# First diff head projected ahead of the remaining differential values, rotary tables placed by transposes, in a two-layer decoder trunk

## The chip, the core and the metric

The kernel runs on one core of a Trainium2 chip. Its engines work side by side, each through its own instructions in order: TensorE (PE) multiplies matrices, VectorE (DVE), ScalarE (ACT) and GpSimd (POOL) do the rest, and SyncE (SP) issues nearly all DMA transfers; ACT can issue transfers too. An engine that waits for another holds up all that stands behind the waiting instruction. The metric is the device time of one execution in microseconds (us).

## The reference, cut to what matters

```
rotary_tables: ang = positions[..., None] * inv_freq          # 8 frequencies
               cos, sin = cos(ang), sin(ang)
partial_rotary(t): t1, t2, rest = t[..., :8], t[..., 8:16], t[..., 16:]
               concat([t1*cos - t2*sin, t2*cos + t1*sin, rest])
for l in range(2):
    h = rms_norm(x, attn_pre_g[l]);  proj = h @ w_in[l]
    qa, ka, va, qb, kb, vb, f_logit = split(proj)
    qa, ka = partial_rotary(qa), partial_rotary(ka)            # 4 diff heads, 2 maps of 64 each
    oa = rms_norm(diff_attention(qa, ka, va, lam), diff_sub_g[l]) * (1 - lam_init)
    ob = forgetting_attention(qb, kb, vb, cumsum(log_sigmoid(f_logit + bias)))   # 8 fox heads
    x = x + rms_norm(concat(oa, ob) @ w_out[l], attn_post_g[l])
    h = rms_norm(x, ffn_pre_g[l])
    x = x + rms_norm((silu(h @ w_gate[l]) * (h @ w_up[l])) @ w_down[l], ffn_post_g[l])
```

x is 512 tokens by 1024, a head has 64 dims, the feed-forward width is 2816; everything is float32.

## The kernel before

Each float32 factor is split into a rounded part `h` and a remainder `l`, and a product is three matmuls, h by h, h by l and l by h. The split costs a copy on ACT (`hi`) and a subtraction on DVE or POOL (`lo`). The normalised input stands transposed in `hT_h` and `hT_l`, in eight blocks `k` of 128 columns.

Layer 0 starts in `start()`. Four token tiles `t` of 128 rows are loaded (`xs`), squared and summed, scaled by POOL's `r_s` (`h_a`, L483), transposed on PE (`hp_a`, L209) in two halves `z` and split into `hT`. Beside that the weights of the differential values `va` come in four chunks `c` of two blocks (`w_load`), and PE computes `va` in 16 pieces (t, c) of six matmuls. `WARM` small matmuls on zeros stand ahead of and between the first pieces. The raw weights lie in the later `mixed_d` and in `raw_v`, the split ones in the places of the first queries and keys (`qs`, `ks` tiles) and of a weight chunk (`wh`, `wl`).

`tables()` makes the rotary tables `cosT` and `sinT`, one row for each of the 128 dims of a map pair: eight loads put the positions (L541), a chain of small DVE instructions on 128 x 32 elements brings the angles into range (L550 to L563), ACT takes the sines (L565, L566), and the result goes to DRAM (`tab_d`, L570) and back into the rows of the tables (L575). It also loads the mask (`con`), the triangle `tu` that becomes `upr`, and the lambda vectors `lv`.

Then come the heads. `tile_chunk` loads and splits the weights of one head's keys or queries (`wr_kd`, `wh_kd`, `wl_kd`; `q` for queries, `f` for a fox pair), projects them on PE (`pj_kd`, 24 matmuls), and for a diff head rotates them: DVE multiplies by `cosT` (t1, L728), shuffles (L732) and multiplies by `sinT` (t2, L735), POOL adds (L738); ACT and DVE or POOL split the sum into `qs` or `ks` (L697, L705, L706), and two transfers copy the key halves (L710). `diff_head` computes scores `sd` (two matmuls each), softmax on DVE, ACT and POOL, transposes `ptd`, and the product with the values `od`. `fox_head` does alike with a decay.

The order is not written by hand in this part. Every step is an `Op` with an engine, an assumed duration, a key and the buffers that it takes and gives; `Plan.run` picks for each engine the ready step with the lowest key, or else the one that can start first, and the instructions are emitted in that order. Projections have the key `FILLER` and so fill PE wherever no step of a head is ready. `va` pieces have the keys

```
done[t, c] = add("P", 1390, vas, hT[t, c // 2] + wl[c] + ([done[t, c - 1]] if c else []),
                 key=500 + VA_C * c + VA_T * t)
```

so that all of them run ahead of any projection. The transfers stand on SP's queue in a fixed order (`order="ld"`), and a transfer that takes over one of eight completion semaphores waits for the transfer that had it before.

Of the kernel before, what the change touches and what calls it, by code (L numbers as in the profile page):

```python
# [34 lines left out]
TB = S // 16  # L35
VA_C, VA_T = 4, 1
# [7 lines left out]
C_ID, C_M, C_F, NKEEP, C_U = 0, 128, 640, 641, 641  # L44
NCONST = 1153
# [113 lines left out]
def _constants():  # L159

    c = np.zeros((P, NCONST), np.float32)
    r = np.arange(P)
    c[:, C_ID:C_ID + P] = np.eye(P, dtype=np.float32)
    c[:, C_U:C_U + P] = (r[None, :] >= r[:, None]).astype(np.float32)
    c[:, C_U + P:C_U + S] = 1.0
    c[:, C_M + S - P:C_M + S] = np.where(r[None, :] > r[:, None], np.float32(-BIG), np.float32(0.0))
    expo = np.arange(0, ROT, 2, dtype=np.float32) / np.float32(ROT)
    inv_freq = (np.float32(1.0) / np.power(np.float32(500000.0), expo).astype(np.float32)).astype(np.float32)
    c[:, C_F] = inv_freq[r // 16]
    return c  # L170
# [3 lines left out]
def hymba_block(ctx, tc, x_d, pos_d, apre_d, win_d, fb_d, lq1_d, lk1_d, lq2_d, lk2_d, dsg_d, wout_d, apost_d,  # L174
# [64 lines left out]
    V.memset(sinT, 0.0)  # L239
    G.memset(cosT, 1.0)  # L240
# [102 lines left out]
    for l in range(DEPTH):  # L343
        win = win_d[l]
        with ExitStack() as actx:
# [12 lines left out]
            mixed_d = ap.tile([P, NDIFF, S], F32, name=f"mixd{l}", tag="v8", bufs=5)  # L358
            if l == 0:
                raw_v = ap.tile([P, NDIFF, S], F32, name=f"rawv{l}", tag="v8", bufs=5)  # L360
# [18 lines left out]
            vd, tab = [], []  # L379
# [12 lines left out]

            def start():

                plan.free.update(g=[], v8=[0.0], qs=[], ks=[])
# [9 lines left out]
                idd = dma(con[:, :P], con_d[:, :P], P)  # L405

                def w_load(c):
                    raw = (mixed_d, raw_v)[c // 2][:, 2 * (c % 2):2 * (c % 2) + 2]
                    if c == 0:
                        dst = q_tile("wva0h"), q_tile("wva0l")  # L410
                    elif c < 3:
                        w = k_tile(f"wva{c}")
                        dst = w[:, 0], w[:, 1]
                    else:
                        dst = [wpool.tile([P, WCH], F32R, name=f"{x}_va3", tag=x).rearrange("p (a b) -> p a b", a=2)
                               for x in ("wh", "wl")]
                    hi, lo = dst
                    d = dma(raw, win[2 * c * P:(2 * c + 2) * P, VA:VA + S].rearrange("(k p) n -> p k n", p=P), 2 * S)
                    ops = []
                    for k in range(2):  # L420
                        wva[2 * c + k] = hi[:, k], lo[:, k]
                        a = add("A", dA(S), lambda k=k: A.copy(hi[:, k], raw[:, k]), [d], key=-85 + c,
                                take=["w"] if c == 3 and k == 0 else [], order="hi w" if c == 3 and k == 0 else "")
# [13 lines left out]
                zeros = sinT.bitcast(mybir.dt.bfloat16)  # L437
# [16 lines left out]
                for t in range(NT):  # L454
# [24 lines left out]
                    for z in range(2):  # L479
# [20 lines left out]
                        p = add("P", 436, tr, [v, idd], key=key, take=["ts"[z]], give=["e"])  # L500
# [3 lines left out]
                for t in range(NT):  # L504
                    for c in range(4):
                        def vas(t=t, c=c):
                            if t == NT - 1:
# [4 lines left out]
                                         key=500 + VA_C * c + VA_T * t)  # L512
                    vd_split(t, [done[t, 3]])
                for c in range(4):
                    add("P", 0, lambda: None, [done[t, c] for t in range(NT)], key=-99,
                        give=(["qs", "qs"], ["ks"], ["ks"], ["w"])[c])
                add("P", 0, lambda: None, wl[2] + wl[3], key=-99, give=["v8"])
                add("P", 0, first_va.clear, [done[t, 0] for t in range(NT)], key=-99)
                return hT[NT - 1, 1]

            def tables(last):

# [3 lines left out]
                tab_d = dpool.tile([4, 8, S], F32, name="tab_d", tag="tabd")  # L526
# [4 lines left out]
                def get(dst, src, n, **kw):  # L531
                    return add("Q", max(400, 1.43 * n), lambda: nc.sync.dma_start(dst(), src), key=1, lat=2000,
                               order="ld" + "".join(f" {k}" for k in kw.get("take", ())), **kw)

                def positions():
                    w = rbuf("rd", F32, "rot")
                    x["p"] = w[:, :TB].bitcast(I32)
                    x["a"], x["n"] = w[:, TB:2 * TB], w[:, 2 * TB:3 * TB]
                    x["t"] = w[:, 4 * TB:8 * TB].rearrange("p (x j) -> p x j", x=4)
                    blocks = pos_d[0].rearrange("(b j) -> b j", j=TB)  # L540
                    return [lambda f=f: nc.sync.dma_start(x["p"][16 * f:16 * f + 16], blocks) for f in range(8)]  # L541

                def sums():
                    x["tu"] = rbuf("rc", F32, "tu")
                    return x["tu"]
# [4 lines left out]
                v = op("V", 100, lambda: V.tensor_copy(x["a"], x["p"]), [dp])  # L550
                v = op("V", 100, lambda: V.tensor_scalar_mul(x["a"], x["a"], con[:, C_F:C_F + 1]), [v, dc])
                for sc in (2.0 ** 22, 2.0 ** 11, 1.0):
                    v = op("V", 100, lambda sc=sc: V.tensor_scalar(
                        x["n"], x["a"], scalar1=1.0 / (2.0 * math.pi * sc), scalar2=MAGIC, op0=ALU.mult,
                        op1=ALU.add), [v])
                    v = op("V", 100, lambda: V.tensor_scalar(x["n"], x["n"], scalar1=-MAGIC, scalar2=1.0, op0=ALU.add,
                                                             op1=ALU.mult), [v])
                    for part in _two_pi_parts():
                        v = op("V", 110, lambda sc=sc, part=part: V.scalar_tensor_tensor(
                            x["a"], x["n"], -part * sc, x["a"], op0=ALU.mult, op1=ALU.add), [v])  # L560
                v = op("V", 100, lambda: V.tensor_scalar(x["a"], x["a"], scalar1=3.1415925, scalar2=-3.1415925,
                                                         op0=ALU.min, op1=ALU.max), [v])
                v = op("V", 110, lambda: V.scalar_tensor_tensor(x["n"], x["a"], -1.0, x["a"], op0=ALU.mult,  # L563
                                                                op1=ALU.max), [v])
                a = op("A", 1500, lambda: A.activation(x["t"][:, 3], x["a"], AF.Sin), [v] + last)  # L565
                c = [op("A", 220, lambda j=j: A.activation(x["t"][:, j], x["n"], AF.Sin, bias=halfpi, scale=-1.0), [a])  # L566
                     for j in range(2)]
                v = op("V", 100, lambda: V.tensor_scalar_mul(x["t"][:, 2], x["t"][:, 3], -1.0), [a])
                p = op("A", 1300, lambda: A.preload_act_table_set("natural_log_exp_and_others"), c)
                d = op("Q", 500, lambda: nc.sync.dma_start(tab_d.rearrange("x f (b j) -> (f b) x j", j=TB), x["t"]),  # L570
                       [v, *c], lat=2000, give=["rd"])
# [78 lines left out]

            last_fill, last_tile = [], []

            def fillers(pieces, deps, take={}, give=()):

                ends = []
                for z, (dur, fn) in enumerate(pieces):
# [676 lines left out]
```

## Time and profile before

| | |
|---|---|
| median of 3 runs | 1262.27 us (1256.56 to 1264.68) |
| profiled execution | 1261.95 us |
| its span, first to last instruction | 1260.1 us |
| PE busy | 1223.8 us (97%) |
| DVE, ACT, POOL busy | 633.0, 520.8, 279.6 us |
| mean granted TensorE clock | 0.993 |

Rows are read as start, duration, engine, source line, operation and tiles; "out<-in" are the program's names without numbers. A bracket at the end of a row tells how long the engine stood idle before it and what ended that. Since PE is busy for 97% of the span, a step matters if it makes PE wait or adds matmuls.

### The profile page before, as it was taken

What the parts mean: (1) busy time and instruction counts of PE and PEld (TensorE: products, weight loads), DVE (VectorE), ACT (ScalarE), POOL (GpSimd) and SP (SyncE); (2) the same over time, 40 slices, a digit from 0 to 9 for tenths busy, and PEclk for the clock granted to TensorE, in tenths of its full rate; (3) what the DMA queues carried; (4) which work ended last, traced back from release to release, by engine and by line L of the source; (5) the groups of instructions that cost most, each with busy time, mean ns of one, the idle gap of its engine ahead of it and who ended that gap; (6) DMA issues with size and microseconds to landing.
All of it is one profiled execution on the core that took longest, in us unless ns stands there. A gap on an engine that the chain in (4) does not pass through costs nothing.

```text
span 1260.1 us, 15914 instructions
## 1 busy us (share of the span) xinstructions
PE 1223.8 (97%) x5949; PEld 1015.2 (81%) x5949; DVE 633.0 (50%) x1188; ACT 520.8 (41%) x1008; POOL 279.6 (22%) x318
## 2 busy tenths in 40 slices
PE   8999999999999999999999999999999999999998
PEld 5788877798888888888877878777988888888886
DVE  7597858563333333222556867685633333332224
ACT  5465757453222222222344647674522222222221
POOL 1555557220000000000246535671100000000001
PEclk9999999999999999999999999999999999999999
DMA  7334343404333334223413333442133333332222
GB/s 241 79 84 111 93 117 103 132 18 117 98 89 98 101 101 131 88 99 106 128 35 93 88 98 93 125 129 81 51 101 100 91 93 101 100 118 87 97 100 84
DMA packets 158717, 125.94 MB, mean 100 GB/s; under 512 B 7008, under 2 KB 134112, under 8 KB 158640
## 3 DMA queue, kind: packets, MB, share of 16 engines
q1 hardware_dynamic: 158496, 124.40, 33.3%
q8 instruction: 47, 0.77, 0.3%
q10 hardware_dynamic: 144, 0.52, 0.1%
q14 instruction: 30, 0.25, 0.1%
HBM read 114.32 MB, written 2.20 MB: 92 GB/s over the span
## 4 chain that ended last, share of the span: by engine, by line
PE 56%; issue 31%; DVE 6%; ACT 3%; POOL 2%; DMA 1%; SPq 0%; POOLq 0%; DVEq 0%; ACTq 0%
PE pj_g L204 10%; PE pj_u L204 10%; PE d L204 9%; PE o L204 4%; PE pj_kd L204 3%; PE pj_qd L204 3%; PE vb L204 3%; PE va L204 3%; PE pj_kf L204 2%; PE pj_qf L204 2%; PE sd L204 2%; PE sf L204 1%; PE ptf L209 1%; PE of L204 1%; DVE ae L1033 1%
## 5 line engine op out<-in xcount | busy, mean ns | idle before, releaser
L204 PE MATMUL pj_g<-hT_h,wh_g 128*128 128x512 f32 (+1 forms) x384 | 142.9, 372 | 0.0
L204 PE MATMUL pj_g<-hT_h,wl_g 128*128 128x512 f32 (+1 forms) x384 | 142.6, 371 | 0.0
L204 PE MATMUL pj_g<-hT_l,wh_g 128*128 128x512 f32 (+1 forms) x384 | 142.6, 371 | 0.0
L204 PE MATMUL pj_u<-hT_h,wh_u 128*128 128x512 f32 (+1 forms) x368 | 140.1, 381 | 0.0
L204 PE MATMUL pj_u<-hT_l,wh_u 128*128 128x512 f32 (+1 forms) x368 | 139.8, 380 | 0.0
L204 PE MATMUL pj_u<-hT_h,wl_u 128*128 128x512 f32 (+1 forms) x368 | 139.8, 380 | 0.0
L204 PE MATMUL d<-wh_d,hh 128*128 128x512 f32 x336 | 130.8, 389 | 0.0
L204 PE MATMUL d<-wl_d,hh 128*128 128x512 f32 x336 | 130.7, 389 | 0.0
L204 PE MATMUL d<-wh_d,hl 128*128 128x512 f32 x336 | 130.7, 389 | 0.0
L258 DVE TENSOR_TENSOR wl_u<-wr_u,wh_u 128x1024 fp32r<-128x1024 f32 x44 | 53.9, 1225 | 150.2 <-ACT wh_u L257 150.2
L258 DVE TENSOR_TENSOR wl_d<-wr_d,wh_d 128x1024 fp32r<-128x1024 f32 x42 | 51.4, 1224 | 146.9 <-ACT wh_d L257 146.5
L257 ACT CAST wh_u<-wr_u 128x1024 fp32r<-128x1024 f32 x44 | 46.3, 1052 | 157.9 <-PE pj_g L204 151.6
L257 ACT CAST wh_d<-wr_d 128x1024 fp32r<-128x1024 f32 x42 | 44.3, 1054 | 157.3 <-PE d L204 134.3
L257 ACT CAST wh_g<-wr_g 128x1024 fp32r<-128x1024 f32 x44 | 46.3, 1053 | 145.8 <-issue 124.7
L1206 DVE TENSOR_TENSOR sg<-pj_u,sg 128x512 f32<-128x512 f32 x44 | 30.4, 692 | 141.7 <-PE pj_u L204 141.7
L270 POOL TENSOR_SCALAR v_fp<-s_fp 128x1 f32<-128x1 f32 x8 | 4.0, 506 | 367.0 <-ACT junk L276 366.7
L204 PEld LDWEIGHTS pj_g<-hT_h,wl_g 128*128 128x128 f32 x384 | 72.4, 188 | 12.6
L204 PEld LDWEIGHTS pj_g<-hT_l,wh_g 128*128 128x128 f32 x384 | 72.3, 188 | 12.5
L204 PEld LDWEIGHTS pj_g<-hT_h,wh_g 128*128 128x128 f32 x384 | 72.3, 188 | 12.4
L204 PEld LDWEIGHTS pj_u<-hT_h,wh_u 128*128 128x128 f32 x368 | 69.3, 188 | 13.1
L204 PEld LDWEIGHTS pj_u<-hT_h,wl_u 128*128 128x128 f32 x368 | 69.1, 188 | 13.1
L204 PEld LDWEIGHTS pj_u<-hT_l,wh_u 128*128 128x128 f32 x368 | 69.2, 188 | 12.9
(272 smaller groups left out, 2768.8 us busy)
## 6 DMA issues: line engine op xcount, KB each, us to landing
wr_g<-in_w_gate_dram SPq DMA_DIRECT2D x44, 512.0 KB, 3.8
wr_u<-in_w_up_dram SPq DMA_DIRECT2D x44, 512.0 KB, 3.8
wr_d<-in_w_down_dram SPq DMA_DIRECT2D x44, 512.0 KB, 3.4
wr_o<-in_w_out_dram SPq DMA_DIRECT2D x16, 512.0 KB, 4.2
wr_kd<-in_w_in_dram SPq DMA_DIRECT2D x8, 512.0 KB, 4.0
wr_qd<-in_w_in_dram SPq DMA_DIRECT2D x8, 512.0 KB, 4.0
ksd<-ksd SPq DMA_DIRECT2D x16, 256.0 KB, 2.9
wr_kf<-in_w_in_dram SPq DMA_DIRECT2D x8, 512.0 KB, 3.8
```

Of the source, the lines that this page charges most:

```text
L204: ins = PE.matmul(out, a, b, start=start, stop=stop)
L209: ins = PE.transpose(out, a, idn)
L257: A.copy(hi, raw)
L258: (eng or V).tensor_sub(lo, raw, hi.bitcast(F32))
L270: G.tensor_scalar(v, s2[:, 0:1], scalar1=s2[:, 1:2], scalar2=EPS, op0=ALU.add, op1=ALU.add)
L1033: return V.tensor_scalar_mul(b["e"][:, :n], b["e"][:, :n], b["l"])
L1206: V.tensor_mul(sg, pu, sg)
```

## The change

The first diff head's projections get the key `FILLER - 40`, and `va` pieces of token tiles 2 and 3 get keys from `FILLER - 20` on (tiles 0 and 1 keep theirs), so that keys and queries of the first head run ahead of what is left of `va`. Since the places of those keys and queries must then be free, the split weights of `va` go to three `v8` tiles and to a weight chunk, the raw ones to the `pt` tiles, and `mixed_d` is allocated once two of the `v8` tiles are done with. The rotary tables are made in the new `rotary()`: one load on ACT's queue brings the positions, one token per partition, four columns; DVE forms 4 x 8 angles with immediate factors and the same range reduction, its steps having key -95, ahead of the normalisations; ACT writes sines and cosines into two zeroed or one-filled tiles `rsin`, `rcos`, PE transposes them, ACT copies them into `sinT` and `cosT`. ACT's table for the sines is loaded at the very start. The warming matmuls read `upr` instead of `sinT`.

```diff
-VA_C, VA_T = 4, 1
+VA_C, VA_T, VA_EARLY = 4, 1, 2
...
-    V.memset(sinT, 0.0)
-    G.memset(cosT, 1.0)
+    V.memset(upr.bitcast(F32), 0.0)
...
             def start():
-                plan.free.update(g=[], v8=[0.0], qs=[], ks=[])
+                plan.free.update(g=[], v8=[], rc=[], rd=[], pt=[])
+                tc.keep_in_program_order(A.preload_act_table_set("trig_and_small"))
...
-                idd = dma(con[:, :P], con_d[:, :P], P)
+                idd.append(dma(con[:, :P], con_d[:, :P], P))
+                rotary()
                 def w_load(c):
-                    raw = (mixed_d, raw_v)[c // 2][:, 2 * (c % 2):2 * (c % 2) + 2]
-                    if c == 0:
-                        dst = q_tile("wva0h"), q_tile("wva0l")
-                    elif c < 3:
-                        w = k_tile(f"wva{c}")
-                        dst = w[:, 0], w[:, 1]
+                    lo = (wv_l0, wv_l1)[c // 2][:, 2 * (c % 2):2 * (c % 2) + 2]
+                    if c < 2:
+                        hi = wv_h0[:, 2 * c:2 * c + 2]
                     else:
-                        dst = [wpool.tile([P, WCH], F32R, name=f"{x}_va3", tag=x).rearrange("p (a b) -> p a b", a=2)
-                               for x in ("wh", "wl")]
-                    hi, lo = dst
+                        x = ("wh", "wl")[c - 2]
+                        hi = wpool.tile([P, WCH], F32R, name=f"{x}_va", tag=x).rearrange("p (a b) -> p a b", a=2)
+                    tag = "pt" + "hl"[c % 2]
+                    raw = ap.tile([P, 10 * P], F32, name=f"rawv{c}", tag=tag, bufs=2)[:, :WCH]
...
-                                         key=500 + VA_C * c + VA_T * t)
+                                         key=(500 if t < VA_EARLY else FILLER - 20) + VA_C * c + VA_T * t)
...
+            def rotary():
+                key = -95
+                w = rbuf("rd", F32, "rot")
+                tabs = [rbuf("rc", F32, n) for n in ("rcos", "rsin")]
+                pos, pf = w[:, :NT].bitcast(I32), w[:, NT:2 * NT]
+                an, nn = (w[:, c:c + 8 * NT] for c in (32, 64))
+                G.memset(tabs[0], 1.0)
+                G.memset(tabs[1], 0.0)
+                v = op("A", 500, lambda: A.dma_start(pos, pos_d[0].rearrange("(j p) -> p j", p=P)), [], lat=3000)
+                v = op("V", 80, lambda: V.tensor_copy(pf, pos), [v])
+                v = op("V", 700, lambda: [lambda f=f, c=c: V.tensor_scalar_mul(an[:, f * NT:(f + 1) * NT], pf, c)
+                                          for f, c in enumerate(_inv_freq())], [v])
...
+                def place(z, half, m):
+                    out = tabs[z].rearrange("p (j r) -> p j r", j=NT)[:, :, HD * m + 8 * half:HD * m + 8 * half + 8]
+                    src = (nn, an)[z].rearrange("p (f j) -> p j f", j=NT)
+                    if z == 0:
+                        return lambda: A.activation(out, src, AF.Sin, bias=halfpi, scale=-1.0)
+                    return lambda: A.activation(out, src, AF.Sin, scale=1.0 if half else -1.0)
+                for z, dep in ((0, v2), (1, v)):
+                    a = op("A", 800, lambda z=z: [place(z, half, m) for half in range(2) for m in range(2)], [dep])
+                    def tr(z=z):
+                        x[z] = (bank_t, bank_s)[z](f"rot{z}")
+                        for j in range(NT):
+                            transpose(x[z][:, j * P:(j + 1) * P], tabs[z][:, j * P:(j + 1) * P], ident)
+                    p = op("P", 436, tr, [a, idd[0]], take=["ts"[z]])
+                    ends.append(op("A", dA(S), lambda z=z: A.copy((cosT, sinT)[z], x[z]), [p], give=["ts"[z]]))
...
             def tables(last):
-                dp = add("Q", 3000, positions, key=1, lat=2000, order="ld rd", take=["rd"])
-                dc = get(lambda: con[:, P:], con_d[:, P:NKEEP], S)
-                du = get(sums, con_d[:, C_U:C_U + S], S, take=["rc"])
...
+                du = add("Q", 1.43 * S, sums, key=1, lat=2000, order="ld rc", take=["rc"])
...
-                last_tile[:] = fillers([(650, piece(k)) for k in range(KT)], [ready], take={0: ["g"]}, give=["w"])
+                last_tile[:] = fillers([(650, piece(k)) for k in range(KT)], [ready], take={0: ["g"]}, give=["w"],
+                                       key=FILLER - 40 if kind == "d" and l == z == 0 else FILLER)
```

What the planner makes of it stands in the built programs. On DVE, at the start, before (`ss_a00` is the read of a row sum, `h_a000` the first normalised half tile, `wva0l` the first weight remainder):

```order
L468 ISA ss_a00_116 128x1
L483 SCALAR_TENSOR_TENSOR h_a000_162<-xs_78,r_s0_117,g_apre0_105 128x512
L483 SCALAR_TENSOR_TENSOR h_a001_153<-xs_78,r_s0_117,g_apre0_105 128x512
L424 TENSOR_TENSOR wva0l_0_107<-mixd0_101,wva0h_0_106 128x512 x2
L498 TENSOR_TENSOR hT_l_80<-hp_a000_169,hT_h_79 128x4x128
```

and the same place on DVE with the change (`rot` holds positions and angles):

```order
L475 ISA ss_a00_122 128x1
L548 CAST rot_0_107<-rot_0_107 128x4
L549 TENSOR_SCALAR rot_0_107<-rot_0_107 128x4 x8
L552 TENSOR_SCALAR rot_0_107<-rot_0_107 128x32
L490 SCALAR_TENSOR_TENSOR h_a000_178<-xs_78,r_s0_123,g_apre0_106 128x512
L554 TENSOR_SCALAR rot_0_107<-rot_0_107 128x32
L490 SCALAR_TENSOR_TENSOR h_a001_159<-xs_78,r_s0_123,g_apre0_106 128x512
L557 SCALAR_TENSOR_TENSOR rot_0_107<-rot_0_107 128x32
L431 TENSOR_TENSOR wvl0_100<-rawv0_112,wvh0_102 128x512
```

The conversion of the positions and ten small instructions moved ahead of the first normalisation, the rest one by one between the large ones.

On PE, around the first head's first scores `sd0000`, before (`pj_qd01` are the second head's queries):

```order
L204 MATMUL pj_qd01_580<-hT_l_80,wh_qd01_496 128x512
L204 MATMUL pj_qd01_580<-hT_h_79,wl_qd01_497 128x512
L204 MATMUL sd0000_607<-ksd0_0_533,qsd0_0_591 128x128 x2
L204 MATMUL sd0001_610<-ksd0_0_533,qsd0_0_591 128x128 x2
L204 MATMUL pj_qd01_580<-hT_h_79,wh_qd01_496 128x512
```

and with the change (`va03` is the last token tile of the values, `pj_kd01` are the second head's keys):

```order
L206 MATMUL va03_121<-wvl1_101,hT_h_79 128x512
L206 MATMUL va03_121<-wl_va_116,hT_l_80 128x512
L206 MATMUL sd0000_569<-ksd0_0_503,qsd0_0_553 128x128 x2
L206 MATMUL sd0001_572<-ksd0_0_503,qsd0_0_553 128x128 x2
L206 MATMUL pj_kd01_575<-hT_h_79,wh_kd01_466 128x512
```

Ahead of the first score stood 16 `va` pieces, both projections of the first head, the second head's keys and 15 of 24 matmuls of its queries; now 10 `va` pieces, both projections of the first head and the other 6 pieces.

On SP, where the first head's weights `wr_kd00` and `wr_qd00` are loaded, before:

```order
L541 DMA rot_0_234<-in_positions_dram 16x32 x8
L532 DMA con_81<-in_constants_dram 128x513
L532 DMA tu_0_281<-in_constants_dram 128x512
L633 DMA wr_kd00_297<-in_w_in_dram 128x8x128
L633 DMA wr_qd00_308<-in_w_in_dram 128x8x128
```

and with the change, where twelve small loads (`lv`, `fbb`, `dsg`) come between `con` and these:

```order
L608 DMA fbb_89<-in_forget_bias_dram 128x8
L609 DMA dsg_90<-in_diff_sub_g_dram 128x1
L593 DMA tu_0_369<-in_constants_dram 128x512
L654 DMA wr_kd00_377<-in_w_in_dram 128x8x128
L654 DMA wr_qd00_392<-in_w_in_dram 128x8x128
```

`tu` now takes over a buffer of the table tiles, so its load, and the two behind it, wait for the transposes on PE.

## Rows read from the trace of the kernel before

**Rows 1.** The page, part 1: busy us, share of the span, instructions.

```profile
PE 1223.8 (97%) x5949; PEld 1015.2 (81%) x5949; DVE 633.0 (50%) x1188; ACT 520.8 (41%) x1008; POOL 279.6 (22%) x318
```

**Rows 2.** Whom PE waited for, 0 to 330 us: total us, times, longest.

```profile
PE hp_a L209 <- DVE h_a L483: 3.8, 2, 3.3
PE sd L204 <- DVE md L871: 3.5, 3, 1.7
PE ptf L209 <- DVE ae L1033: 2.5, 2, 1.9
PE sd L204 <- issue: 1.5, 1, 1.5
```

**Rows 3.** The chain that ended last, 0 to 130 us: start, us, what.

```profile
20.80 0.88 PE hp_a L209 x8
21.67 16.37 PE va L204 x72
38.04 5.44 PE pj_kd L204 x24
43.48 5.44 PE pj_qd L204 x24
```

**Rows 4.** Stages: us, busy of PE, PEld, DVE, ACT, POOL, clock, DMA share, GB/s.

```profile
10.00:15.00 5.00, 4.46 (x26) 2.71 (x24) 4.67 (x8) 4.97 (x14) 1.63 (x3) 1.00 1.02 389
```

**Rows 5.** Instructions in order of time, 0 to 26 us: start, us, engine.

```profile
0.72 0.41 ACTq L403 DMA_DIRECT2D g_apre<-in_attn_pre_g_dram  x1
1.15 1.28 ACT L464 ACT_TABLE_LOAD   x1 [1.15 <-PEq L1322]
5.68 0.38 SPq L399 DMA_DIRECT2D rawv<-in_w_in_dram  x1
6.98 0.08 DVE L468 DVE_READ_ACCUMULATOR2_ANT ss_a<- 128x1 f32 x1
7.33 8.92 SPq L541 DMA_DIRECT2D rot<-in_positions_dram  x8
8.24 1.41 DVE L483 SCALAR_TENSOR_TENSOR h_a<-xs,r_s,g_apre 128x512 f32<-128x512 f32 x2 [1.17 <-POOL r_s L391]
22.59 1.28 DVE L498 TENSOR_TENSOR hT_l<-hp_a,hT_h 128x512 fp32r<-128x512 f32 x2
23.96 1.06 ACT L641 CAST wh_qd<-wr_qd 128x1024 fp32r<-128x1024 f32 x1 [0.59 <-DMA wr_qd<-in_w_in_dram]
24.39 1.22 DVE L645 TENSOR_TENSOR wl_kd<-wr_kd,wh_kd 128x1024 fp32r<-128x1024 f32 x1
```

**Rows 6.** DMA issues: KB each, median us to landing.

```profile
wr_kd<-in_w_in_dram SPq DMA_DIRECT2D x8, 512.0 KB, 4.0
tab_d<-rot SPq DMA_DIRECT2D x1, 64.0 KB, 1.8
```

**Rows 7.** Instructions in order of time, 27 to 33 us: small ones.

```profile
27.78 0.64 DVE L559 SCALAR_TENSOR_TENSOR rot<-rot 128x32 f32<-128x32 f32 x3
32.21 0.53 ACT L566 ACTIVATE rot<-rot,halfpi 128x32 f32<-128x32 f32 x2
```

**Rows 8.** Instructions in order of time, 39 to 60 us: the first head.

```profile
39.25 2.39 POOL L645 TENSOR_TENSOR wl_kd<-wr_kd,wh_kd 128x1024 fp32r<-128x1024 f32 x1 [19.88 <-ACT wh_kd L641]
47.48 1.29 POOL L738 TENSOR_TENSOR t1kd<-t1kd,t2kd 128x512 f32<-128x512 f32 x1 [0.63 <-DVE t2kd L735]
49.50 3.00 POOL L706 TENSOR_TENSOR ksd<-t1kd,ksd 64x512 fp32r<-64x512 f32 x2 [0.73 <-ACT ksd L697]
56.26 1.26 ACT L697 CAST qsd<-t1qd 64x512 fp32r<-64x512 f32 x2 [0.99 <-POOL t1qd L738]
57.04 2.79 DVE L705 TENSOR_TENSOR qsd<-t1qd,qsd 64x512 fp32r<-64x512 f32 x2
59.21 0.41 PE L204 MATMUL sd<-ksd,qsd 128*128 128x128 f32 x2 [1.46 <-issue]
```

**Rows 9.** A stage behind the fox heads, columns as in rows 4.

```profile
230.00:231.00 1.00, 1.00 (x3) 0.72 (x3) 0.63 (x3) 0.96 (x3) 0.00 (x0) 0.50 0.47 132
```

More of the change, by code (lines that the diff above doesn't have):

```diff
@@ L356, in k_tile @@
                 return ap.tile([P, 2, 2, S], F32R, name=f"{nm}_{l}", tag="ks", bufs=2)
-            mixed_d = ap.tile([P, NDIFF, S], F32, name=f"mixd{l}", tag="v8", bufs=5)
             if l == 0:
-                raw_v = ap.tile([P, NDIFF, S], F32, name=f"rawv{l}", tag="v8", bufs=5)
+                wv_l0, wv_l1, wv_h0 = (ap.tile([P, NT, S], F32R, name=n, tag="v8", bufs=5)
+                                       for n in ("wvl0", "wvl1", "wvh0"))
+            else:
+                mixed_d = ap.tile([P, NDIFF, S], F32, name=f"mixd{l}", tag="v8", bufs=5)
             vd_h = ap.tile([P, NT, S], F32R, name=f"vdh{l}", tag="v8", bufs=5)
@@ L422, in w_load @@
                         a = add("A", dA(S), lambda k=k: A.copy(hi[:, k], raw[:, k]), [d], key=-85 + c,
-                                take=["w"] if c == 3 and k == 0 else [], order="hi w" if c == 3 and k == 0 else "")
+                                take=["w"] if c == 2 and k == 0 else [], order="hi w" if c == 2 and k == 0 else "")
                         ops += [a, add("V", dV(S) + 80, lambda k=k: V.tensor_sub(
@@ L517, in start, with mix @@
-                add("P", 0, lambda: None, wl[2] + wl[3], key=-99, give=["v8"])
+                def mix():
+                    nonlocal mixed_d
+                    mixed_d = ap.tile([P, NDIFF, S], F32, name=f"mixd{l}", tag="v8", bufs=5)
+                add("P", 0, lambda: None, sum(wl.values(), []), key=-99, give=["pt", "pt"])
+                half, full = ([done[t, c] for t in range(NT)] for c in (1, 3))
+                add("P", 0, lambda: None, half, key=-99, give=["v8", "v8"])
+                add("P", 0, lambda: None, full, key=-99, give=["v8", "w"])
@@ L525, in tables @@
                 x = {}
-                tab_d = dpool.tile([4, 8, S], F32, name="tab_d", tag="tabd")
                 def op(eng, dur, fn, deps, **kw):
                     return add(eng, dur, fn, deps, key=key, **kw)
[L531 to L541, printed above, removed]
@@ L552, in tables @@
[L552 to L560, printed above, removed]
@@ L561, in tables @@
[L561 to L571, printed above, removed]
-                rows = tab_d.rearrange("x f s -> (x f) s")
-                for T, r0 in ((cosT, 0), (sinT, ROT)):
-                    for m in (0, HD):
-                        tab.append(op("Q", 400, lambda T=T, r0=r0, m=m: nc.sync.dma_start(
-                            T[m:m + ROT], rows[r0:r0 + ROT]), [d], lat=2000))
+                    return nc.sync.dma_start(x["tu"], con_d[:, C_U:C_U + S])
@@ L577, in tables @@
+                tab.append(add("Q", 1.43 * S, lambda: nc.sync.dma_start(con[:, P:], con_d[:, P:NKEEP]), key=1, lat=2000,
+                               order="ld"))
+                du = add("Q", 1.43 * S, sums, key=1, lat=2000, order="ld rc", take=["rc"])
+                p = op("A", 1300, lambda: A.preload_act_table_set("natural_log_exp_and_others"), last + tab)
                 tab.append(p)
```

52 lines of the change are left out of this document (33 added, 19 removed).

## The prediction

> **What bounds the kernel now.** The page comes first [rows 1]: TensorE (PE) is busy 1223.8 of 1260.1 us, so PE idles 36 us in all, and no other engine is above 50%. The change touches layer 0 alone, from its start to its diff heads; in the planned order of the fox heads, the feed-forward part and layer 1 nothing moves. So the next view is who PE waits for in the first 330 us [rows 2]: 3.8 us for the first normalised rows (line L483), then for the scores `sd` of the diff heads 3.5 us on VectorE (DVE) and 1.5 us of "issue" ahead of the first one, then 2.5 us at the end of the fox heads. The chain that ended last [rows 3] shows the stretch between: from 21.67 us the value projection `va` runs without a break, followed by the key and query projections `pj_kd` and `pj_qd`, 24 matmuls in 5.44 us each, 0.227 us a matmul. Up to the first score PE has no hole: what is put ahead or behind there changes no sum, and whatever PE does more, or starts later, is paid in full. What feeds PE before 22 us is DVE, busy 4.67 of the 5 us from 10 to 15 us [rows 4]. So the start is bound by DVE until PE has its first chunks, then by PE.
>
> **The change part by part.** The sum is made against the profiled execution: 1261.95 us, of which 1260.1 are the span and 1.85 lie around it; the median of the three runs is 0.3 us above it.
>
> *Positions.* Before, eight loads of the positions held the SP queue for 8.92 us from 7.33 us, and DVE came to them only after 25 us. Now one load of 512 single elements is issued by ScalarE (ACT), behind the table load and behind the gain row `g_apre`, and DVE waits for it in fourth place, ahead of the first normalisation. DVE was ready there at 7.06 us (the read of `ss_a`, 6.98 + 0.08), and the first normalisation began at 8.24 us, on POOL's `r_s` [rows 5]. When does the load land? `g_apre` was issued at 0.72 us, and the `rawv` load that takes over its semaphore went out at 5.68 us: 4.96 us for it under a full DMA load. The table load of 1.28 us now goes first on ACT, so `g_apre` lands at about 7.0 us. For the positions the nearest row is `tab_d`, 64 KB in as many pieces (512), which took 1.8 us from issue to landing with the DMA engines nearly idle [rows 6]. Lower end: 1.8 us after an issue at 2.9 us, 4.7 us, before DVE gets there: nothing lost. Upper end: behind everything that the other queue holds; the DMA share is 1.02 until 15 us [rows 4], so 15 us. I take the same queue's order, 1.8 us behind `g_apre` alone and twice that if every second turn goes to the other queue: 8.8 to 10.6, middle 9.7 us.
> The Trainium skill (DMA: Bandwidth & Descriptors, section Queues, rings and completion order) says that a DMA engine takes turns between the queues by whole packets of some 9 to 17 descriptors, not one by one. No row here shows single turns; by it some 32 elements per engine would pass in two to four turns, an estimate that ends nearer to 8.8 us, and the sum below would be about 1 us lower.
> After the landing come a conversion, eight multiplications and one more small instruction. Dependent small ones took 0.64 us for three [rows 7], 0.21 each; independent ones less. I take 1.1 us for the ten. The first normalisation then starts at 10.8 us instead of 8.24: **+2.6 us** (0 to +7.8).
>
> *The rest of the angle work on DVE.* 16 more small instructions stand singly between the normalisations and splits of the start, where DVE is full; before, they ran at 27 to 32 us beside PE's `va`. Up to the second chunk of `va` there are 8 of them: from 0.07 (hidden behind a big neighbour's tail) to 0.21 us each, 0.6 to 1.7, taken **+1.0 us**. Those behind it cost nothing as long as PE has chunks: the last `hT_l` stood at 23.87 us (22.59 + 1.28) [rows 5]; DVE now has 2.6 + 2.4 (tiny ones) + 0.64 (one more split ahead) + 1.2 (the `lv` sums ahead) more to do, so 30.7 us, and PE wants it at 34.6 us (below).
>
> *Transposes and tables.* Eight transposes of the cosine and sine tables are new on PE: 0.88 us by the row of eight `hp_a` [rows 3], with one more warming matmul **+1.1 us**. Eight activations and two copies are new on ACT; the round trip through DRAM (store and four loads, after 32 us) and one table load of 1.28 us go. That side had slack: the tables were wanted at 43.5 us, when `pj_kd` had ended. The other places of the weights and the later `mixd` tile change no load and no split, only when a buffer comes free: 0.
>
> *Keys and queries first.* Before, the first score stands behind 16 chunks of `va`, two pairs of projections but nine matmuls; now behind 16 chunks and one pair, with 39 matmuls fewer ahead (8.8 us). Those 39 now lie between the scores: PE's work is the same, and the gain can only be stalls that vanish. Ten chunks run first, so PE reaches `pj_kd` at 38.04 - 6 x 1.36 + 1.1 + 3.6 = 34.6 us. Call its end T = 40.0. Before, the first score waited 1.46 + 0.31 us, and it came 10.3 us after its queries' last matmul (48.92 to 59.21) [rows 3, 8]. Now POOL has in a row: the second keys' weights 2.39, rotary sum 1.29, key split 3.00, the second queries' weights 2.39, rotary sum about 1.3, together 10.4 us from T + 1.2; then 1.27 on ACT and 0.7 to 2.8 on DVE (the 2.79 us of [rows 8] lay beside POOL work): T + 13.6 to T + 15.7. PE arrives at T + 5.44 + 8.16 = T + 13.6. A stall of 0 to 2.1 us, taken 1.0, in place of 1.8: **-0.8 us**.
> Behind it stand the waits of later scores, 3.5 us in three places [rows 2]. The lead melts: in the new order the second head's scores stand 2.8 us of PE work later than before, the third head's about 1 us later, the last diff head's 2 us earlier, and from the first fox head on the order is the same but for the 1.1 us. DVE at 9 of 10 us does the same work there, plus the second keys' rotation and two value splits that used to come before the first score. So I take away little: **-0.5 us** (-3.5 to +2).
>
> Sum: 2.6 + 1.0 + 1.1 - 0.8 - 0.5 = +3.4 us, 1265.4, rounded to **1265 us**.
>
> **The rivals.**
> *A, the lead counts.* Positions land before DVE gets there, and the first head's earlier start takes the score waits away: 0 + 0.6 + 1.1 - 1.8 - 3.5 = -3.6 us, 1258. For it: three of the waits on [rows 2] lie in the diff heads, which now start 39 matmuls earlier. Against it: DVE is full there, and the second head gains nothing.
> *B, late positions (slower).* The place is DVE's fourth instruction, the price 1 us for each us that the load lands after about 7 us, since everything in the start stands behind it on DVE. At 15 us it is +7.8 instead of +2.6. The granted clock adds to it: near 230 us, after a wait of 1.9 us in a stretch of many waits, it stood at 0.50, the lower level of 1.2 GHz [rows 9], whereas the 3.3 us of waiting at 9 us [rows 2] left it at 1.00 (2.4 GHz); about 8 us of waiting may well not, and three us at half clock lose 1.5. Sum: 3.4 + 5.2 + 1.5 = +10, 1272.
> *C, it doesn't come first.* The first keys' weights are now queued on SP behind the load of `tu`, which waits until PE has transposed the sine table out of the buffer. By rows: the angles are ready at 10.8 + 15 x 0.64 + 2 = 22.4, four activations of 0.27 [rows 7] 23.5, transposes 23.9, two issues 24.8, landing 4.0 [rows 6] 28.8, ACT 1.06 and DVE 1.22 [rows 5]: 31.1 us against PE's 34.6. It decides only if that path is 3.5 us longer than this. With a slow load and late angles together, PE waits some 2 to 4 us with six chunks locked behind `pj_kd`: 1268.
>
> **How the numbers follow.** My forecast, 1262 to 1269, has 0.5; A (1254 to 1262) 0.22; B (1269 to 1276) 0.15; C (1266 to 1270) 0.13. The three runs of before already lie 8 us apart, so 1% (12.6 us, 1249.6 to 1274.9 on the median) is about what a measurement can tell from no change. The range from 1256 to 1273 leaves out the far ends of A and B, about 0.2. Faster by over 1% would need more than all PE waits of the diff and fox heads together: 0.03. Slower by over 1% needs B at its end: 0.06. Within 1%: 0.91.
>
> **What would show it.** DVE's conversion at line L548 should wait for the position load until 9 to 11 us, and the first normalisation begin near 10.8; right for A if it begins before 8.5, for B after 13. PE should reach `pj_kd` near 34.6 us with no wait (a wait there speaks for C), and the first score should stand near 54.6 us, against 59.21, with a wait of about 1 us. The fox heads and layer 1 should show the same waits as before. The forecast is wrong if the score waits vanish altogether, or if the granted clock falls in the first 30 us.

## The result and the profile after

The changed kernel takes 1279.45 us (median of 4 runs, 1275.25 to 1281.43), beside 1261.02 us of the kernel before in the same comparison: ratio 1.0136, 95% interval 1.011 to 1.0162. By the ratio it is slower by 17 us or 1.4% (the medians lie 18.4 us apart), outside the forecast range (1256 to 1273). The profiled execution took 1275.25 us, its span is 1273.5 us against 1260.1, 13.4 us more.

Part 1 of the page, after:

```profile
PE 1239.3 (97%) x5958; PEld 1011.3 (79%) x5958; DVE 630.0 (49%) x1194; ACT 521.7 (41%) x1014; POOL 280.9 (22%) x319
```

Against [rows 1] PE is busy 15.5 us longer, with nearly the same instructions. PE's idle time is 34.2 us, where it was 36.3: the loss is not in waits. Whom PE waited for from 0 to 330 us, after (total us, times, longest):

```profile
PE ptd L211 <- DVE ed L975: 3.5, 3, 2.0
PE hp_a L211 <- DVE h_a L490: 2.5, 2, 1.7
PE ptf L211 <- DVE ae L1055: 2.4, 2, 1.9
PE va L206 <- DVE upr L241: 1.4, 1, 1.4
PE ptd L211 <- DVE ptld L940: 1.3, 1, 1.3
PE sd L206 <- DMA ksd<-ksd: 1.0, 1, 1.0
```

The waits of the scores [rows 2] have gone over to the transposes `ptd` of the probabilities; the wait at the end of the fox heads is as it was. The start, after, in order of time:

```profile
0.71 1.28 ACT L401 ACT_TABLE_LOAD   x1 [0.71 <-PEq L1344]
...
0.75 0.40 ACTq L409 DMA_DIRECT2D g_apre<-in_attn_pre_g_dram  x1
1.18 0.45 ACTq L547 DMA_DIRECT2D rot<-in_positions_dram  x1
...
6.73 0.16 DVE L548 CAST rot<-rot 128x4 f32<-128x4 int32 x1
6.93 0.67 DVE L549 TENSOR_SCALAR rot<-rot 128x4 f32<-128x4 f32 x8
...
8.06 0.75 DVE L490 SCALAR_TENSOR_TENSOR h_a<-xs,r_s,g_apre 128x512 f32<-128x512 f32 x1 [0.25 <-POOL r_s L394]
```

Against [rows 5], ACT's queue issued both loads beside the table load, not behind it. The positions were there when DVE came to them, and the first normalisation began 0.2 us earlier than before. The chain that ended last, 20 to 60 us and then in the gate stage, after:

```profile
22.46 0.87 PE rot L211 x8
...
25.16 6.99 PE va L206 x30
32.15 5.67 PE pj_kd L206 x24
37.82 5.60 PE pj_qd L206 x24
...
51.95 0.46 PE sd L206 x2
...
309.90 5.60 PE pj_g L206 x24
315.50 5.60 PE pj_u L206 x24
```

And the same view of the gate stage before:

```profile
308.88 5.44 PE pj_u L204 x24
314.31 5.44 PE pj_g L204 x24
```

Here is the loss. The order did what it should: the keys are projected at 32.15 us instead of 38.04, the first score stands at 51.95 instead of 59.21 [rows 3, 8]. But 24 matmuls take 5.60 us where they took 5.44. From the start of one matmul to the start of the next, which is called the pitch here, that is 233.3 ns instead of 226.7, in the feed-forward part 250 us behind the change. The grouping of PE's instructions by form shows which matmuls (busy us, mean ns). Before:

```profile
L204 PE MATMUL d<-wh_d,hh 128*128 128x512 f32 x336 | 130.8, 389 | 0.0
...
L204 PE MATMUL pj_g<-hT_h,wh_g 128*128 128x512 f32 x320 | 124.5, 389 | 0.0
```

After:

```profile
L206 PE MATMUL d<-wh_d,hh 128*128 128x512 f32 x336 | 130.8, 389 | 0.0
...
L206 PE MATMUL pj_g<-hT_h,wh_g 128*128 128x512 f32 x320 | 126.4, 395 | 0.0
```

(A matmul's own time, 389 ns, is longer than the pitch, since neighbours overlap.) All 512-column matmuls that read `hT` became slower, gate and up alike; the down projection `d` did not. From the first `pj_g` of layer 0 to the first `d` it took 242.1 us before (267.9 to 510.0) and 248.2 after (274.3 to 522.5): 6.1 us more, and as much in layer 1. By the pitch, 984 matmuls times 6.7 ns are 6.6 us a layer.

The granted clock does not explain it. In the gate stage it was 1.00 in both kernels, as these windows show (clock behind the engines' busy times); PE is busy throughout, with 928 matmul records in 210 us before and 915 after:

```profile
290.00:500.00 210.00, 210.00 (x928) 173.95 (x927) 72.84 (x78) 60.94 (x78) 0.00 (x0) 1.00 0.35 103
```

```profile
290.00:500.00 210.00, 210.00 (x915) 169.29 (x914) 71.03 (x76) 60.27 (x77) 0.00 (x0) 1.00 0.34 98
```

Over the whole span the clock speaks the other way. In the kernel before it fell to the lower level (0.50, 1.2 GHz) four times ahead of the end, in the changed kernel once. One fall of each, before and after:

```profile
228.00:234.00 6.00, 4.52 (x15) 3.65 (x16) 4.45 (x13) 2.83 (x8) 1.25 (x1) 0.72 0.60 172
```

```profile
108.00:114.00 6.00, 5.02 (x17) 4.09 (x18) 5.22 (x17) 2.79 (x11) 2.78 (x1) 0.72 0.29 79
```

A mean of 0.72 over 6 us is a loss of 6 x 0.28 = 1.7 us. Without its falls the kernel before would have a span of 1260.1 - 6.8 = 1253.3 us, the changed one 1273.5 - 1.7 = 1271.8. Read like that the change costs 18.5 us in this pair of executions.

### The profile page after: what moved, and what is told of

Its sections match the earlier page's. It is cut to its first block, busy times and chain, and to the rows that moved or that the text cites. A ratio compares the mean times of both kernels' runs of the same rounds, so it can differ in the third digit from the quotient of the medians.

```text
span 1273.5 us, 15914 instructions
## 1 busy us (share of the span) xinstructions
PE 1239.3 (97%) x5958; PEld 1011.3 (79%) x5958; DVE 630.0 (49%) x1194; ACT 521.7 (41%) x1014; POOL 280.9 (22%) x319
## 4 chain that ended last, share of the span: by engine, by line
PE 55%; issue 31%; DVE 6%; ACT 4%; POOL 2%; DMA 1%; SPq 0%; POOLq 0%; DVEq 0%; ACTq 0%
PE pj_g L206 10%; PE pj_u L206 10%; PE d L206 9%; PE o L206 5%; PE pj_kd L206 4%; PE pj_qd L206 3%; PE va L206 2%; PE pj_kf L206 2%; PE vb L206 2%; PE pj_qf L206 2%; PE ptf L211 1%; PE sd L206 1%; PE od L206 1%; PE of L206 1%; PE sf L206 1%
## 5 line engine op out<-in xcount | busy, mean ns | idle before, releaser
L206 PEld LDWEIGHTS pj_u<-hT_h,wh_u 128*128 128x128 f32 x368 | 69.0, 188 | 15.5
L206 PEld LDWEIGHTS pj_u<-hT_h,wl_u 128*128 128x128 f32 x368 | 69.0, 187 | 15.4
```

The lines of the kernel that those rows point to most:

```text
L206: ins = PE.matmul(out, a, b, start=start, stop=stop)
```

## The experiments

**Theory A: addresses.** The angles' factors are now immediate, so the change takes one column from `con`:

```
-C_ID, C_M, C_F, NKEEP, C_U = 0, 128, 640, 641, 641
+C_ID, C_M, NKEEP, C_U = 0, 128, 640, 640
```

In the built programs tiles are placed at multiples of 32 bytes of a partition, so `con` goes from 2592 to 2560 bytes, and all that is allocated behind it stands 32 bytes lower: the weights' tiles `wh`, `wl`, the attention's and the feed-forward part's own tiles. `hT_h` and `hT_l` stand ahead of `con` and stay. A matmul has a stationary operand (a 128 x 128 block, which PEld loads ahead of it) and a moving one (here 512 columns). For a gate matmul the distance of the stationary operand (the weights) from the moving one (`hT`) changes by 32 bytes; for `d` both operands moved. **Theory B:** the new order of the start, or the clock, made the matmuls slow. None of the four kernels below changes an instruction's work or the order on any engine.

*a_shift_back*, the changed kernel with its tiles back at the old places:

```
     con = cpool.tile([P, NKEEP], F32, name="con")
+    cpool.tile([P, 1], F32, name="gap")
```

> The changed kernel with one unused tile of 4 bytes a partition put behind con, which moves every tile allocated after con up by 32 bytes, back to where the kernel before has them (the weights' tiles wh and wl at 0 modulo 64 instead of 32). Nothing else moves. Theory A (addresses: the changed kernel lost its time because con became 32 bytes shorter): the 512-column matmuls of the projections go from 395 ns back to 389 ns, the gate and up stages of both layers from about 248 to 242 us, TensorE's busy time from 1239 to about 1224 us, and the time from 1279 to 1260-1266 us. Theory B (the new order of the start, or the clock, made the matmuls slow): the matmuls stay at 395 ns and the time at 1275-1281 us.

1269.01 us (1265.82 to 1271.22, 6 runs), ratio to before 1.0059 (1.0039 to 1.0079). The matmuls are back:

```profile
L206 PE MATMUL pj_g<-hT_h,wh_g 128*128 128x512 f32 x320 | 124.5, 389 | 0.0
```

By the ratios about 10 us of the loss are the places; the falls of the clock blur this figure, and the last paragraphs of this section take them out. The time stays 3 us above the range that was expected; the rest is taken up below.

*b_shift32*, the same line in the kernel before:

> The kernel before with the same unused tile behind con: every tile after con moves up by 32 bytes, so that the weights stand at 32 modulo 64 while the activations hT_h and hT_l stay at 0 modulo 64; no instruction changes. Theory A (addresses): projections' 512-column matmuls 389 -> 395 ns, TensorE busy +15 us, time 1261 -> 1273-1279 us. Theory B (order of the start): no change, 1257-1265 us and 389 ns.

1278.44 us, ratio 1.013 (1.011 to 1.0149): without any of the change, its whole loss.

```profile
L204 PE MATMUL d<-wh_d,hh 128*128 128x512 f32 x336 | 130.8, 389 | 0.0
...
L204 PE MATMUL pj_g<-hT_h,wh_g 128*128 128x512 f32 x320 | 126.6, 396 | 0.0
```

*b_all32*, the kernel before with the unused tile behind `xs`, ahead of `hT`, so that `hT` moves along:

> The kernel before with the unused tile behind xs: activations hT_h and hT_l and everything after them move up by 32 bytes, so that activations and weights all stand at 32 modulo 64. Theory A in its first form (what counts is how the weights stand against the activations; the down projection, both of whose operands moved in the changed kernel, kept 389 ns): as before, 389 ns and 1257-1265 us. Theory A in its second form (what counts is each address by itself modulo 64): at least as slow as the shift behind con alone, 395 ns or more, 1273-1290 us. Theory B (order of the start): 1257-1265 us.

1264.44 us, ratio 1.002 (1.0004 to 1.0035), and 389 ns:

```profile
L204 PE MATMUL pj_g<-hT_h,wh_g 128*128 128x512 f32 x320 | 124.5, 389 | 0.0
```

So, for these shifts, it is not the address of either operand but their distance. Its clock fell six times by 1.7 us; 1263.6 less 10.2 is 1253.4, the kernel before less its falls to 0.1 us.

*a_wpool32*, the changed kernel with `PAD` 112 instead of 104:

> The changed kernel with the pad behind the weight pool 32 bytes longer (PAD 104 -> 112): the weights wh and wl stay where the changed kernel has them (32 modulo 64), the attention's and the feed-forward part's own tiles (differential values' weights, wo1, probabilities, hidden rows) go back to 0 modulo 64. Theory A with the weights' tiles as the cause: gate and up stay at 395 ns and 248 us a layer, time 1272-1281 us, at most 2-4 us given back by o and va matmuls whose operands are in the attention's pool. Theory A with the other tiles as the cause: back to 389 ns, 1260-1266 us. Theory B: 1275-1281 us, 395 ns everywhere.

1287.76 us, ratio 1.0209 (1.0191 to 1.0226), 8 us above the changed kernel, which neither theory had expected as I wrote them down. I had taken both operands of `d` to be in the feed-forward part's pool. The stationary `hh` is, the moving `wh_d` is in the weights' pool, and the longer pad pulled them apart by 32 bytes:

```profile
L206 PE MATMUL d<-wh_d,hh 128*128 128x512 f32 x336 | 133.0, 396 | 0.0
...
L206 PE MATMUL pj_g<-hT_h,wh_g 128*128 128x512 f32 x320 | 126.4, 395 | 0.0
```

This is the distance again, on a second pair of tiles. Theory B has fallen: the matmuls follow the places in both kernels, under either order.

**How far the distance counts.** *m_pitch* leaves the block out and issues only groups of 32 matmuls, the stationary operand s and the moving one m bytes behind a multiple of 128:

```
for k in range(n):
    a, b = (k % 8) * P + s // 4, (k % 4) * WIDE + m // 4
    nc.tensor.matmul(ps[:, :cols], sta[:, a:a + P], mov[:, b:b + cols], start=k == 0, stop=k == n - 1)
```

> A kernel that leaves the whole block out and only issues groups of 32 matmuls (128x128 stationary, 512 moving columns, with three groups of 256) whose stationary operand starts s bytes and whose moving operand m bytes behind an address that is 0 modulo 128; each group twice. Theory A (what counts is the distance of the two addresses modulo 64): pitch 227 ns where s-m is 0 modulo 64 (0/0, 64/0, 128/0, 0/64, 16/16, 32/32), about 232-233 ns at a distance of 32, and for the distances 4 to 24 either the same or a middle value. Theory A in its other form (each address by itself): 32/32 and 16/16 slow as well. If the effect needs the whole kernel (other engines' traffic): 227 ns everywhere. [...]

Some groups by tile (s and m in the name, `w` 512 columns, `h` 256; ns min/median/max):

```profile
L203 PE MATMUL s0m0wa<-mov,sta x32: 387/392/402, 38.9 to 46.0; 128*128 128x512 f32 x32
L203 PE MATMUL s32m0wa<-mov,sta x32: 392/394/398, 75.9 to 83.1; 128*128 128x512 f32 x32
L203 PE MATMUL s48m16wa<-mov,sta x32: 388/390/391, 164.6 to 171.6; 128*128 128x512 f32 x32
L203 PE MATMUL s0m0ha<-mov,sta x32: 279/281/283, 171.9 to 175.5; 128*128 128x256 f32 x32
L203 PE MATMUL s32m0ha<-mov,sta x32: 278/281/284, 175.7 to 179.3; 128*128 128x256 f32 x32
```

Inconclusive as a test of 64 bytes: at distance 0 single matmuls took 387 to 402 ns, and 48/16, a distance of 32, was the fastest group. My moving rows lay 2176 bytes apart, not 2048 as in the kernel, so the distance changed from matmul to matmul by an odd multiple of 128 bytes, and 64 could not be the whole rule. It did show that the effect needs no other engine. With 256 columns the groups at 0 and 32 took the same time, 281 ns; in the whole kernel the 256-column `pj_g` took 288 ns before and 285 after.

*m_pitch2* takes the strides, the order and, modulo 4096, the base addresses of the gate stage; 48 matmuls a group:

```
for z in range(2 * KT):
    k = z % KT
    for n, (wl, hl) in enumerate(((0, 0), (0, 1), (1, 0))):
        a, b = wl * 3 * WCH + k * P + s // 4, hl * KT * S + k * S + m // 4
```

> A kernel that leaves the whole block out and only issues groups of 48 projection matmuls in the order and with the strides of the gate stage (stationary chunks 512 bytes apart, moving rows 2048 bytes apart, base addresses the same modulo 4096 as those of hT_h and wh in the kernel before), the stationary operand s and the moving one m bytes further. In the first such kernel the strides differed and the pitch depended on the address pair of every single matmul (388 to 398 ns). Theory A (the distance modulo 64, for these strides): 389 ns at s-m = 0, 64, 128, 192, 256 and at 16/16 and 32/32, 395 ns at a distance of 32, whether the weights or the activations are moved; 4 to 16 and 48: open. If the strides decide alone: the same duration in all groups.

In order of time (start, us of the group):

```profile
42.01 11.05 PE L205 MATMUL s0m0wa<-mov,sta 128*128 128x512 f32 x48
86.32 11.35 PE L205 MATMUL s32m0wa<-mov,sta 128*128 128x512 f32 x48
108.71 11.35 PE L205 MATMUL s64m0wa<-mov,sta 128*128 128x512 f32 x48
142.29 11.15 PE L205 MATMUL s192m0wa<-mov,sta 128*128 128x512 f32 x48
153.29 11.05 PE L205 MATMUL s256m0wa<-mov,sta 128*128 128x512 f32 x48
186.50 11.15 PE L205 MATMUL s0m64wa<-mov,sta 128*128 128x512 f32 x48
197.49 11.25 PE L205 MATMUL s16m16wa<-mov,sta 128*128 128x512 f32 x48
208.58 11.05 PE L205 MATMUL s32m32wa<-mov,sta 128*128 128x512 f32 x48
```

With the last matmul's 0.39 us taken off and 47 pitches, 11.05 us are 226.8 ns and 11.35 us 233.2: the kernel's own two values. The expectation of 64 bytes fell. Fast are distances of 0 and 256; 64 is slow if the weights move, and the same distance modulo 256 gives the same time by either operand (weights 192 further, or activations 64 further: 11.15). 16/16 is at distance 0 and slower all the same (231.1), so where the operands start counts too: in this measurement fast were only starts at multiples of 32. The slowest group was 96/0, with 234.2 ns. No pair tried was faster than 226.7. Distance alone is not the whole rule: in the strides of *m_pitch* the fast group 48/16, with 226.7 ns, starts at a distance of 32, which no rule here explains.

*b_shift64* and *b_wpool256* try the period in the whole kernel. The first puts `[P, 16]` instead of `[P, 1]` behind `con`, the second `[P, 64]`, with `PAD` 40 instead of 104, so that the weights move by 256 bytes and the tiles of the attention and the feed-forward part not at all.

> The kernel before with an unused tile of 64 bytes a partition behind con: everything after con, the weights among it, stands 64 bytes further, the activations stay. Theory A with the period 64 bytes: 389 ns and 226.7 ns of pitch in the gate and up stages, time 1257-1266 us as before. Theory A with a longer period (128 bytes or more): 392-396 ns, 1268-1279 us.

1276.41 us, ratio 1.0123 (1.0065 to 1.0181):

```profile
L204 PE MATMUL pj_g<-hT_h,wh_g 128*128 128x512 f32 x320 | 126.6, 396 | 0.0
```

> The kernel before with 256 unused bytes behind con and the pad behind the weight pool 256 bytes shorter: the weights' tiles stand 256 bytes further from the activations, all tiles of the attention and feed-forward parts stay. Theory A with the period 256 bytes (as the measurement of groups by itself gave: 389 ns at distances 0 and 256, 392-397 ns at every other distance tried): 389 ns, 1256-1266 us as before. If any shift of the weights costs (so that the shifts by 32 and 64 were no matter of a period): 394-396 ns and 1273-1279 us.

1259.70 us, ratio 0.9983 (0.9965 to 1.0):

```profile
L204 PE MATMUL pj_g<-hT_h,wh_g 128*128 128x512 f32 x320 | 124.5, 389 | 0.0
```

In gate and up 64 bytes cost what 32 cost, and 256 cost nothing. In the kernel before, weights, hidden rows and values all stood at a multiple of 256 bytes from `hT` (by the addresses in the built program, 74624 - 32896 = 163 x 256 for `wh`).

**The rest: order or tables.** a_shift_back is still 5 to 10 us over the kernel before. *c_order_old* and *c_early3* keep its places and undo the order, wholly or by half:

```
-VA_C, VA_T, VA_EARLY = 4, 1, 2
+VA_C, VA_T, VA_EARLY = 4, 1, 4        # c_early3: 3, and nothing else
...
-  key=FILLER - 40 if kind == "d" and l == z == 0 else FILLER)
+  key=FILLER)
```

> The changed kernel with the addresses put back (as in a_shift_back) and, of the change, the first head's keys and queries no longer ahead of the remaining values (VA_EARLY 2 -> 4, the first head's tile at FILLER again): TensorE's order is that of the kernel before but for the 8 table transposes; the tables by transposes and the values' weights' new places stay. a_shift_back stands at 1269.0 us, 8 us over the kernel before. Theory A (the rest of the loss is the new order: less work left beside the first heads' softmax, so that later transposes and scores wait): the first score near 58-60 us, waits of TensorE from 60 to 150 us back from 7.7 to about 4.5 us, time 1260-1264 us. Theory B (the rest of the loss is the tables: transposes on TensorE, small instructions on VectorE in the start): time 1267-1271 us.

> As a_shift_back, but three quarters of the differential values instead of half are computed ahead of the first head's keys and queries (VA_EARLY 2 -> 3). Theory A (the order costs): between a_shift_back and the old order, 1263-1268 us. Theory B (the tables cost): 1267-1271 us as a_shift_back.

c_order_old: 1262.83 us (12 runs), ratio 1.0017 (0.9994 to 1.004). c_early3: 1264.79 us (12 runs), 1.0034 (1.0014 to 1.0054). a_shift_back had 1.0059: the more values are put behind the first head, the slower, though neighbours in this row overlap and only its ends are clearly apart. On the medians the tables and the weights' other places cost about 2 us (-1 to 5) against the kernel before, and the order most of the rest. PE's longest waits from 0 to 128 us, c_order_old:

```profile
PE hp_a L211 <- DVE h_a L490: 3.2, 2, 2.8
PE sd L206 <- DVE md L892: 3.0, 2, 1.8
PE pj_kd L206 <- DVE vf L812: 2.1, 1, 2.1
```

and a_shift_back:

```profile
PE ptd L211 <- DVE ed L975: 5.5, 4, 2.0
PE hp_a L211 <- DVE h_a L490: 2.1, 1, 2.1
```

With the new order PE waits for the probabilities on DVE, with the old for the scores' maxima. In all it waits 11.9 us in the first 128 us with the old order and 10.7 with the new, so these waits do not carry the difference. The expectation for c_order_old was wrong on this: from 60 to 150 us PE waited 6.8 us instead of 4.5, and the first score stood at 61.1 us instead of 58 to 60. By the first `pj_kf` (125.2 and 126.5 us, before 119.6) both kernels are late, but 3.4 us of that are two falls of the clock in each. By the first `pj_g` the loss of the new order stands whole: less the falls until then it starts at 270.7 us in a_shift_back and at 267.6 in c_order_old, against 266.2 before. So it arises in the attention of layer 0; which of PE's intervals there carries it stays open. The falls of the clock make such single profiles hard to compare, which the last run looked at.

*a_shift_back2* is the same kernel again:

> The kernel of a_shift_back once more. In its first profile the granted clock fell to half for 3.4 us six times, in the kernel before four times, in the changed kernel once; each such fall costs about 1.7 us. Theory A (the steady loss of the new start is about 4 us, the falls come and go between executions): another count of falls, with the span less 1.7 us a fall again near 1257.4 us; over the kernel before by 3-8 us. Theory B (the new order itself brings two more falls): six falls again, 1267-1271 us.

1267.56 us, ratio 1.0052 (1.0031 to 1.0073). Its three falls, as windows:

```profile
8.00:14.00 6.00, 4.83 (x19) 3.45 (x19) 5.24 (x15) 4.73 (x11) 1.20 (x3) 0.72 1.04 402
96.00:102.00 6.00, 4.88 (x23) 4.66 (x24) 4.53 (x18) 2.65 (x11) 0.87 (x2) 0.72 0.34 87
688.00:692.00 4.00, 4.00 (x15) 3.63 (x15) 2.27 (x11) 3.10 (x10) 3.64 (x4) 0.57 0.00 1
```

Three instead of six: the falls come and go between executions of one kernel. Less its falls the span is 1259.2 us, the first time 1257.4: 4 to 6 us over the kernel before. Falls near 11 and 98 us stood in both profiles of this kernel and not in that of the kernel before; whether the order brings them is open, since b_all32 and b_wpool256 had one near 11 us without it, and the changed kernel, with the same order, had a higher mean clock (0.996 in its 4 runs) than the kernel before (0.994 in 65).

**The falls taken out of every run.** For each run, not only the profiled ones, the span and the mean granted clock are on record. Their product is an estimate of the span without falls; it takes all lost clock as lost time, since PE is busy for 97% of the span, and the clock's three digits leave about 0.6 us of error in a run. For the kernel before it is 1251.4 us on the mean of 65 runs, the same to 0.1 us in all four comparisons, and the runs scatter by 1.7 us (standard deviation) instead of 2.9. Over these 1251.4 us lie, with 95% intervals:

| kernel | runs | us more |
|---|---|---|
| changed kernel | 4 | 20.6 ± 3.9 |
| a_shift_back and a_shift_back2 | 13 | 5.2 ± 1.0 |
| a_wpool32 | 4 | 26.9 ± 2.9 |
| c_early3 | 12 | 3.2 ± 0.9 |
| c_order_old | 12 | 0.7 ± 1.4 |
| b_shift32 | 4 | 16.5 ± 2.6 |
| b_shift64 | 4 | 14.6 ± 2.4 |
| b_all32 | 10 | 0.5 ± 1.2 |
| b_wpool256 | 10 | -0.4 ± 1.1 |

So the places cost 15.4 us (± 3.7) in the changed kernel and 16.5 in the kernel before, the same within the noise. The new order costs 4.5 us (± 1.6), nearly all of the rest, and the tables with the weights' other places cost nothing that these runs can tell. No version tried is faster than the kernel before.

## Why the prediction was wrong

The step that failed is its second sentence on bounds: "The change touches layer 0 alone, from its start to its diff heads; in the planned order of the fox heads, the feed-forward part and layer 1 nothing moves." The order held, and the waits of the fox heads are the same. But the 1968 wide matmuls of gate and up and over a thousand of the projections, in both layers, got a 3% longer pitch from the one column less in `con`, which the prediction does not mention; the other places of the weights it put at 0 because they change "only when a buffer comes free", and it did not ask where a tile lies. No rival held it. In the profiles, less the falls of the clock, it is worth 12 to 17 us (the changed kernel against the two profiles with its tiles put back: 14.4 and 12.6; b_shift32 against the kernel before: 1270.0 - 1253.3 = 16.7), of which 12.2 stand in the gate and up stages.

The sum without it was +3.4 us; with the tiles put back the runs give 5.2 less the falls, 6 to 8 on the medians. That the sum comes so near is luck, for two of its terms were off by 2.6 and 3.9 us and nearly cancel:

- *Positions*, +2.6: measured 0. L548 ran at 6.73 us without a wait. The load did not stand behind the table load, since ACT's queue issued it at 1.18 us, not near 2.9. It then took 5.2 us to land, where the sum had 6.8 (9.7 - 2.9).
- *Small angle work* +1.0 and *transposes* +1.1: the transposes took 0.87 us. PE reached `pj_kd` at 32.15 us, not 34.6. Ten chunks earlier than before without any cost is 38.04 - 8.16 = 29.9, so both terms and a longer pitch of `va` together are 2.3 us, where the prediction had 2.1: about the right size.
- *First score*, -0.8: it stands at 51.95 us instead of the 54.6 expected; with the places put back it waited 0.5 us where 1.0 was taken. The right mechanism, about the right size.
- *Later waits*, -0.5 (-3.5 to +2): wrong in sign. With the places put back PE waited 7.7 us from 60 to 150 us, 5.5 of it `ptd` for `ed`, against 4.3 before (the 3.5 of [rows 2] and 0.8 in small ones): +3.4, paid in part by the shorter waits of the start. The prediction saw that the lead melts; that the transposes would be late next, it did not ask.
- Of rival A the first half held: the positions were early, and the first normalisation began at 8.06 us, ahead of the 8.5 that was its sign. The second half did not: the waits changed place instead of vanishing. C (late first keys) did not happen, `pj_kd` had no wait. A loss larger than B's came from elsewhere: the positions were not late, and the clock did not fall in the first 30 us of the changed kernel's profile.

## What to carry to other kernels

Before a change is costed by what it moves in order, look at what it moves in memory: one constant column less, and every tile behind it stands elsewhere. If a kernel has odd pads, keep the distances between the operands of its main matmuls when a tile ahead of them changes size, and compare the mean ns of one untouched matmul form before and after: 389 against 395 tells it in one row. A moved order should be tried with the places held fixed, or the two effects cannot be told apart. And where the granted clock of each run is known, take it out before comparing runs that lie a few us apart.

## What the runs showed of the hardware

In the strides of the gate stage the pitch of 512-column float32 (fp32r) matmuls, each with a load of its own stationary operand, depends on the places of the two operands in SBUF. With both starts at multiples of 32 bytes it was 226.7 to 226.9 ns at distances of 0 and 256 bytes and 228.8 to 234.2 ns at the others tried, with or without other engines at work; in the kernel, at a granted clock of 1.00, it was 226.7 and 233.3. Outside this frame the rule is not known: 16/16 took 231.1 ns at distance 0, and 48/16 took 226.7 ns at a distance of 32 in other strides. With 256 columns no loss was seen (281 ns at distances 0 and 32, and 288 against 285 ns in the kernel). The loads of the stationary operand run beside the matmul before (188 ns each in both kernels); that the two reads collide is a guess that no run here tried.

The Trainium skill (TensorE: Matmul & The Clock Gate, section Back-to-back issue gap) gives the gap between matmuls by the columns alone: for 512 of them about 131 ns in a stream of loads and matmuls, and by N/2.4 + 2.5 ns about 216 ns for isolated ones. The traces do not agree: no group of the second measurement came below 226.7 ns, and which of 226.7 and 233.3 it was in the kernel was decided by the addresses, so the measurement stands.

ACT's queue issued DMA transfers at 0.75 and 1.18 us while ACT was loading its table from 0.71 to 1.99 us.
